# A fourth buffer for the weights' halves of a two-layer decoder trunk, with room from the descriptors' area and an ordering line for the casts

## The chip, the cores and the metric

The kernel runs on one core of a Trainium2 chip. The metric is the device time of one execution in microseconds. A core has five engines that work side by side, each through its own queue in order: PE (matrix multiplication), ACT (activations, copies, casts), DVE (elementwise work), POOL (elementwise work and the transfers that it issues) and SP (which here only issues transfers). An instruction that must wait for another engine waits for a semaphore, and holds what is queued behind it.

## The reference

Two identical layers over 512 tokens of width 1024. Each layer mixes tokens in four ways and adds the gated sum to x, then adds a SwiGLU block:

```python
def reference(x, positions, ln1, ln2, w_in, ...):
    cos, sin = rotary_tables(positions)
    for l in range(DEPTH):
        h = rms_norm(x, ln1[l])
        x = x + mixer_block(h, cos, sin, w_in[l], ...)
        h = rms_norm(x, ln2[l])
        x = x + swiglu(h, w_ffn_in[l], w_ffn_out[l])
    return x
```

`mixer_block` projects h to the inputs of a forgetting attention (fox), a gated linear attention (gla), a retention (ret) and a state-space scan (ssd) and to four gates; each mixer's result goes through an up projection, is multiplied by the sigmoid of its gate, and the sum goes through `w_out`. `swiglu` has a hidden width of 2816. All of it is float32.

## The kernel before, in words

**Precision.** A float32 product is made of three matmuls in a faster 32-bit format (`mm3`, L202): each operand is split into a high part, its cast, and a low part, the remainder. `split` (L213) does it with a cast on ACT (L214) and a subtraction on DVE (L215). The result is high by high, high by low and low by high.

**The stream of weights.** The weights lie in memory in the order of their use, cut into slabs of eight 128x128 blocks (a slab is 128x1024). `load` (L247) has SP transfer a slab into a tile `wr` (two buffers). `convert` (L259) splits it into `wh` and `wl`, tiles of the pool `wp` that `piece` (L158) makes: three buffers each. `ahead` and `block` (L270, L275) keep the conversion two slabs ahead of use: when PE's program reaches the first block of slab m, slab m+1 is converted, and slab m-1 is given up. The cast into `wh` of a slab has to wait for PE's last matmul on the slab three before, whose buffer it takes. A slab of full-width products is 24 matmuls of 512 columns.

**The stages of a layer.** A group of projections and the state-space, gla, ret and fox mixers come first. The mixers are generators (`ssd`, `gla`, `ret`, `fox`); between their steps `drain` inserts projections, gates and up projections from the list `fill`, so that PE has other work while ACT and DVE do a mixer's elementwise steps. `headnorm` ends gla and ret: squares, split, two matmuls with a constant matrix (tiles `mx` from `cr`), then Ln and Exp on ACT. In fox, `value` transposes the probabilities (L1082), splits them and multiplies them by the values. `ups` (L1163) multiplies an up projection by its gate on DVE (L1171). The second half of a layer is a Strassen scheme for the SwiGLU's input projection (`strassen`): `prep` makes the halves of a product's left operand with tiles from the same `wh` and the pool `lp`, `early` (L1286) makes a low part by a negated copy on ACT (L1289) and an accumulating transfer that POOL issues (L1290), and `collect` copies results out of a bank on ACT (L1352). The plain output projection follows in the slabs' way.

**What sets the order.** The code is recorded once, and then a scheduler puts each engine's instructions into an order, by dependences and by a cost model of its own (`schedule_with_timeline_sim=True`). `order(a, b)` (L222) adds a dependence that only this scheduler sees: a is put behind b in its reckoning, with no semaphore between them. It is used so far for activations and the loads of their tables.

**Memory.** At address 0 of every partition lies an area for the descriptors of POOL's transfers, 16384 bytes by default. The pools follow, `cp` first, then a gap, `wp`, a gap, and the rest. `piece` shifts a tile within its buffer for some slabs.

Of the kernel before, what the change touches and what calls it, by code (L numbers as in the profile page):

```python
# [11 lines left out]
F32R = mybir.dt.float32r  # L12
# [6 lines left out]
P = 128  # L19
# [16 lines left out]
SLAB = 8  # L36
# [98 lines left out]
def trunk(ctx: ExitStack, tc: tile.TileContext, keys, qkeys, xin, pos, wst, wsq, par, ext, cst, out):  # L135
    nc = tc.nc
    V, A, G, T = nc.vector, nc.scalar, nc.gpsimd, nc.tensor
# [3 lines left out]
    wp = ctx.enter_context(tc.tile_pool(name="wp", bufs=3))  # L141
# [9 lines left out]
    def nm(s):  # L151
        uid[0] += 1
        return f"{s}{uid[0]}"
# [2 lines left out]
        pool.tile([P, n // 4], F32, tag=nm("pad"), name=nm("pad"))  # L156

    def piece(tag, shift=0):  # L158
        t = wp.tile([P, SLAB * P + 64], F32R, tag=tag, name=nm(tag))
        return t[:, shift:shift + SLAB * P]  # L160

    pools = {}
# [34 lines left out]
        return ap.rearrange("p (c t) -> p c t", c=n)  # L197

    def mm(o, l, r, start, stop):
        T.matmul(o, lhsT=l, rhs=r, start=start, stop=stop, skip_group_check=True)  # L200

    def mm3(o, l, r, start, stop):  # L202
        (lh, ll), (rh, rl) = l, r
        mm(o, lh, rh, start, False)
        mm(o, lh, rl, False, False)
        mm(o, ll, rh, False, stop)
# [4 lines left out]
            mm(o, a, b, start and i == 0, stop and i == 1)  # L211

    def split(src, hi, lo):  # L213
        A.copy(out=hi, in_=src)  # L214
        V.tensor_tensor(out=lo, in0=src, in1=hi.bitcast(F32), op=ALU.subtract)  # L215
        return hi, lo

    def split_tile(t):
        return split(t, TT(F32R), TT(F32R))

    def split_small(t, shape, tag):
        return split(t, sp.tile(shape, F32R, tag=tag + "h", name=nm(tag), bufs=1), sp.tile(shape, F32R, tag=tag + "l", name=nm(tag), bufs=1))  # L222

    seen = {"set": None, "last": None}

    def order(a, b):
        tc.add_manual_dep(a.ins, b.ins.name, mybir.DependencyInfo(mybir.DependencyClass.NoSync, mybir.DependencyReason.DATA), reason="table")
# [13 lines left out]
            seen["last"] = i  # L241
        return i

    raw, ready = [], []
    cap = [SLABS]

    def load():  # L247
# [7 lines left out]
    def halves(n):  # L255
        w = SLAB * P
        return [slice(0, w // 2), slice(w // 2, w)] if n < 2 else [slice(0, w)]

    def convert():  # L259
        n = len(ready)  # L260
        if n < SLABS:
            far = n % (BLOCKS // SLAB) in TOKEN
            hi, lo = (piece("wh", 16), piece("wl", 48)) if far else (piece("wh"), piece("wl"))
            for h in halves(n):
                split(raw[n][:, h], hi[:, h], lo[:, h])
            ready.append((hi, lo))
            raw[n] = None

    def ahead(n):
        while len(ready) < min(SLABS, cap[0], n):  # L270
            if len(raw) == len(ready):
                load()
            convert()

    def block(*key, width=1):  # L275
        n = len(keys)
        if n % SLAB == 0:
            ahead(n // SLAB + AHEAD)
            if n // SLAB:
                ready[n // SLAB - 1] = None  # L280
        for i in range(width):
            keys.append(key[:-1] + (key[-1] + i * P,))
        i = n % SLAB
        hi, lo = ready[n // SLAB]
        sl = slice(i * P, (i + width) * P)
        return hi[:, sl], lo[:, sl]
# [139 lines left out]
    def group(name, l, cols, src, nk, hook=None):  # L426
        ps = [MX() for _ in cols]
        for k in range(nk):
            if hook and k == 4:
                hook()  # L430
            for i, c in enumerate(cols):
                mm3(ps[i], block(name, l, k, c), src[k], k == 0, k == nk - 1)
        return ps

    def proj(name, l, c, src, nk):
        ps = MM()
        for k in range(nk):
            mm3(ps, block(name, l, k, c), src[k], k == 0, k == nk - 1)
        return ps

    def layer(l, n1, scope):
# [72 lines left out]
        def tokmajor(dst, c, stacked=False):  # L514
            st = {}

            def go(half):
                def f():
                    if half == 0:
                        if not stacked:  # L520
                            dst.append(vp.tile([P, NB, 256], F32, tag="v", name=nm("v")))
                        st["ps"] = [MM(), MM()]
                    for k in range(4 * half, 4 * half + 4):
                        w = block("w_in", l, k, c, width=2)
                        assert (len(keys) - 1) // SLAB % (BLOCKS // SLAB) in TOKEN
                        for tb in range(NB):
                            ts = slice(tb * P, (tb + 1) * P)
                            o = st["ps"][tb // 2][:, (tb % 2) * 256:(tb % 2) * 256 + 256]
                            mm3(o, (n1.hi[:, k, ts], n1.lo[:, k, ts]), w, k == 0 and tb % 2 == 0, k == KD - 1)
                    if half:  # L530
                        for tb in range(NB):
                            v, rt = st["ps"][tb // 2][:, (tb % 2) * 256:(tb % 2) * 256 + 256], n1.rt[:, tb:tb + 1]
                            if stacked:
                                t = TT(F32R).rearrange("p (h s d) -> p h s d", h=NH, s=2)
                                v = v.rearrange("p (h d) -> p h d", h=NH)
                                act(out=t[:, :, 0], in_=v, func=AF.Copy, scale=rt)
                                V.scalar_tensor_tensor(out=t[:, :, 1], in0=v, scalar=rt, in1=t[:, :, 0].bitcast(F32), op0=ALU.mult, op1=ALU.subtract)
                                dst.append(t)
                            else:
                                act(out=dst[0][:, tb], in_=v, func=AF.Copy, scale=rt)  # L540
                return f
            return [(4.1, go(0)), (4.1, go(1))]
# [713 lines left out]
        def strassen(units):  # L1256
# [29 lines left out]
            def early(u, p):  # L1286
                t, j = st[u][OF[p]]
                lo = piece("wl", 32)
                A.activation(out=lo, in_=t, func=AF.Copy, scale=-1.0)  # L1289
                G.dma_start(out=lo, in_=wsq[j], accum_op=ALU.add)  # L1290
                st[u]["lo", p] = lo

            def prep(u, p):
                s = st[u]
                hi = piece("wh")
                if p in LATE:
                    A.copy(out=hi, in_=s[OF[p]][0])
                    s[p] = hi, s.pop(("lo", p))
                    return
                a11, a12, a21, a22 = (s[q][0] for q in ("11", "12", "21", "22"))  # L1300
                if p == 6:
                    s1 = wp.tile([P, SLAB * P], F32, tag="wr", name=nm("wr"), bufs=2)
                    s["s1"] = sub(s1, a21, a22, ALU.add)
                    sub(a21, a11, a21)
                    sub(a11, s1, a11)
                    s[p] = split(a11, hi, LT())
                    if u + 1 < len(units):
                        load(u + 1)
                    return
                if p == 3:  # L1310
                    sub(a12, a12, a11)
                t = {5: s["s1"], 7: a21, 3: a12}[p]
                s[p] = split(t, hi, LT())
# [139 lines left out]
    o, w = PAR_OFF["ln1"]  # L1453
# [78 lines left out]
```

## Time and profile before

| | |
|---|---|
| median of the runs shown (3) | 1709.49 us (1709.37 to 1709.84) |
| profiled execution | 1709.5 us |
| its span in the profile | 1707.8 us |
| granted TensorE clock, mean | 1.0 |
| busy: PE, DVE, ACT, POOL | 99%, 71%, 51%, 13% |

Durations are those of one profiled execution. A view of waits names the engine and line that waited, then what it waited for, the total, the count and the longest. A view of groups names line, engine, operation and tiles (out<-in, buffer numbers left out), then count, busy time, mean of one in ns, and the idle time before it. Matmuls overlap in the profile: the end of each is modelled, so idle time of PE is counted only from that end on. Lines are those of the kernel before; in the changed kernel they are up to three higher.

### The profile page before, as it was taken

The numbers are of one execution on the slowest core, as the hardware profiler recorded it, in microseconds if no ns is written. First come the engines' busy times: TensorE is split into PE (matmuls) and PEld (weight loads), VectorE is DVE, ScalarE is ACT, GpSimd is POOL, SyncE is SP. The second block draws the span as 40 slices with busy tenths as digits, with TensorE's granted clock in tenths as the row PEclk, the third lists the DMA queues.
The fourth block names the chain that finished last, engine by engine and source line by source line (L and its number), as shares of the span: only waits on it lengthen the run. The fifth ranks groups of instructions, "written<-read, shape, count | busy, mean of one in ns | idle before, by whom it ended". The sixth has DMA issues, their size and how long they took to land.

```text
span 1707.8 us, 25188 instructions
## 1 busy us (share of the span) xinstructions
PE 1695.8 (99%) x10164; PEld 1475.3 (86%) x10164; DVE 1215.3 (71%) x1691; ACT 863.5 (51%) x1190; POOL 216.8 (13%) x221
## 2 busy tenths in 40 slices
PE   8999999999999999999999999999999999999998
PEld 7878888888888999998988788888888889999997
DVE  6867676768677677676777666767776677767666
ACT  5435543546347646464544354435554474655643
POOL 3021220022101010101020212201221010101010
PEclk9999999999999999999999999999999999999999
DMA  5322222222235657575333222222222365665753
GB/s 206 100 74 75 75 87 75 87 87 74 88 110 141 193 133 188 136 184 120 92 100 111 73 75 75 90 81 89 76 85 87 99 177 160 152 176 139 186 105 105
DMA packets 54693, 195.00 MB, mean 114 GB/s; under 512 B 6064, under 2 KB 6448, under 8 KB 54576
## 3 DMA queue, kind: packets, MB, share of 16 engines
q1 hardware_dynamic: 45072, 160.45, 29.9%
q0 software_dynamic: 8640, 31.46, 10.4%
q8 instruction: 79, 1.29, 0.3%
q10 hardware_dynamic: 864, 1.48, 0.2%
q14 instruction: 38, 0.31, 0.1%
HBM read 191.28 MB, written 2.10 MB: 113 GB/s over the span
## 4 chain that ended last, share of the span: by engine, by line
PE 96%; DVE 1%; ACT 1%; DMA 1%; issue 0%; ACTq 0%; DVEq 0%
PE mm L200 65%; PE mx L200 31%; PE mx L1082 1%; DMA x<-in_x_dram 0%; DMA t<-in_ext_dram 0%; ACT wh L214 0%; DVE wl L215 0%; PE mx L692 0%; DVE t L372 0%; ACT L233 0%; DVE t L836 0%; ACT g L238 0%; DVE t L1171 0%; PE mx L954 0%; PE mx L871 0%
## 5 line engine op out<-in xcount | busy, mean ns | idle before, releaser
L214 ACT CAST wh<-wr 128x1024 fp32r<-128x1024 f32 (+1 forms) x240 | 250.1, 1043 | 359.8 <-PE mm L200 207.5
L200 PE MATMUL mm<-xh,wh 128*128 128x512 f32 (+1 forms) x1184 | 428.4, 362 | 1.4 <-DVE t L1171 0.9
L200 PE MATMUL mm<-xh,wl 128*128 128x512 f32 (+1 forms) x1184 | 427.5, 361 | 0.0
L200 PE MATMUL mm<-xl,wh 128*128 128x512 f32 (+1 forms) x1184 | 427.5, 361 | 0.0
L215 DVE TENSOR_TENSOR wl<-wr,wh 128x1024 fp32r<-128x1024 f32 (+1 forms) x220 | 285.6, 1300 | 110.3 <-ACT wh L214 108.0
L200 PEld LDWEIGHTS mm<-xh,wh 128*128 128x128 f32 x1184 | 222.4, 188 | 36.3 <-DVE t L1171 1.8
L200 PEld LDWEIGHTS mm<-xl,wh 128*128 128x128 f32 x1184 | 222.4, 188 | 34.4 <-issue 1.5
L200 PEld LDWEIGHTS mm<-xh,wl 128*128 128x128 f32 x1184 | 222.5, 188 | 33.8 <-issue 0.6
L200 PE MATMUL mm<-t,wh 128*128 128x512 f32 x448 | 140.3, 392 | 0.0
L200 PE MATMUL mx<-xh,wh 128*128 128x256 f32 (+1 forms) x448 | 136.1, 311 | 3.1 <-ACT wh L214 3.1
L200 PE MATMUL mx<-xl,wh 128*128 128x256 f32 (+1 forms) x448 | 138.3, 309 | 0.0
L1290 POOL DMA_DIRECT2D wl<-in_wsq_dram x60 | 52.0, 867 | 517.4 <-ACT wl L1289 416.4
L200 PE MATMUL mx<-f,wh 128*128 128x512 f32 x352 | 108.2, 390 | 0.0
L200 PE MATMUL mm<-f,wh 128*128 128x512 f32 x352 | 105.9, 389 | 0.0
L200 PEld LDWEIGHTS mm<-t,wh 128*128 128x128 f32 x448 | 83.2, 188 | 17.3
L215 DVE TENSOR_TENSOR l<-rq,wh 128x1024 fp32r<-128x1024 f32 x60 | 73.2, 1220 | 33.0 <-ACT wh L214 18.6
L200 PEld LDWEIGHTS mx<-xh,wh 128*128 128x128 f32 x448 | 84.0, 188 | 9.3 <-ACT wh L214 4.2
L200 PE MATMUL mx<-xh,wl 128*128 128x256 f32 (+1 forms) x288 | 91.0, 327 | 0.0
L200 PEld LDWEIGHTS mx<-xl,wh 128*128 128x128 f32 x448 | 84.1, 188 | 5.1
L200 PE MATMUL mm<-t,wl 128*128 128x512 f32 x224 | 87.4, 390 | 0.0
L214 ACT CAST wh<-rq 128x1024 fp32r<-128x1024 f32 x60 | 63.0, 1049 | 43.8 <-PE mm L200 21.5
L200 PEld LDWEIGHTS mm<-f,wh 128*128 128x128 f32 x352 | 66.1, 188 | 13.5
(275 smaller groups left out, 3428.6 us busy)
## 6 DMA issues: line engine op xcount, KB each, us to landing
wr<-in_wst_dram SPq DMA_DIRECT2D x216, 512.0 KB, 3.5
rq<-in_wsq_dram SPq DMA_DIRECT2D x60, 512.0 KB, 5.6
wl<-in_wsq_dram POOLq DMA_DIRECT2D x60, 512.0 KB, 6.8
wr<-in_wsq_dram SPq DMA_DIRECT2D x20, 512.0 KB, 6.8
out_dram<-x SPq DMA_DIRECT2D x8, 256.0 KB, 2.0
x<-in_x_dram SPq DMA_DIRECT2D x3, 512.0 KB, 6.7
wr<-in_wst_dram SPq DMA_DIRECT2D x4, 256.0 KB, 5.6
x<-in_x_dram SPq DMA_DIRECT2D x2, 256.0 KB, 4.5
```

Source lines behind the costliest of these rows:

```text
L200: T.matmul(o, lhsT=l, rhs=r, start=start, stop=stop, skip_group_check=True)
L214: A.copy(out=hi, in_=src)
L215: V.tensor_tensor(out=lo, in0=src, in1=hi.bitcast(F32), op=ALU.subtract)
L1082: T.transpose(ps[:, W:W + P], zs[qb][:, kb * P:(kb + 1) * P], ident)
L1290: G.dma_start(out=lo, in_=wsq[j], accum_op=ALU.add)
```

## The change

`wh` and `wl` get four buffers, which takes 2 x 4352 = 8704 bytes more of each partition; the descriptors' area falls from 16384 to 8192 bytes. A slab's cast now takes the buffer of the slab four before, so its semaphore wait is for that slab. In place of the shorter distance, `convert` adds a dependence of the cast on the last matmul recorded before slab n-2 was begun (kept in `spent`) by `order`, which the scheduler alone sees.

```diff
     def piece(tag, shift=0):
-        t = wp.tile([P, SLAB * P + 64], F32R, tag=tag, name=nm(tag))
+        t = wp.tile([P, SLAB * P + 64], F32R, tag=tag, name=nm(tag), bufs=4)
...
     def mm(o, l, r, start, stop):
-        T.matmul(o, lhsT=l, rhs=r, start=start, stop=stop, skip_group_check=True)
+        seen["mm"] = T.matmul(o, lhsT=l, rhs=r, start=start, stop=stop, skip_group_check=True)
...
-        A.copy(out=hi, in_=src)
+        seen["copy"] = A.copy(out=hi, in_=src)
...
-    raw, ready = [], []
+    raw, ready, spent = [], [], {}
...
             for h in halves(n):
                 split(raw[n][:, h], hi[:, h], lo[:, h])
+                if n - 3 in spent:
+                    order(seen["copy"], spent[n - 3])
...
             if n // SLAB:
                 ready[n // SLAB - 1] = None
+                spent[n // SLAB - 1] = seen["mm"]
...
-    nc = _bacc.Bacc("TRN2", target_bir_lowering=False, num_devices=1)
+    nc = _bacc.Bacc("TRN2", target_bir_lowering=False, num_devices=1, dynamic_dma_scratch_size=8192)
```

The scheduler gives every engine but POOL and SP a largely different order. Three places follow.

ACT at the end of retention in layer 0. Before (wh_2883 is the cast of a slab's high part, t_2736 to t_2744 are the squares of a head norm of the retention and their high parts):

```order
L238 ACTIVATE t_2730<-t_2288 128x512
L214 CAST wh_2883<-wr_2881 128x1024
L214 CAST t_2732<-t_2730 128x512
L238 ACTIVATE t_2736<-t_2335 128x512
L214 CAST wh_2921<-wr_2919 128x1024
L214 CAST t_2738<-t_2736 128x512
```

And now:

```order
L238 ACTIVATE t_2742<-t_2382 128x512
L214 CAST t_2744<-t_2742 128x512
L238 ACTIVATE t_2748<-t_2438 128x512
L214 CAST t_2750<-t_2748 128x512
L238 ACTIVATE t_2815<-mx_2803,cs 128x512
L238 ACTIVATE t_2817<-mx_2806,cs 128x512
L214 CAST wh_2883<-wr_2881 128x1024
L238 ACTIVATE t_2815<-t_2815 128x512
L214 CAST wh_2921<-wr_2919 128x1024
```

The cast of wh_2883 moved from ahead of the second square's high part to behind the activations that read the sums mx_2803 and mx_2806.

PE at the same place, now (mm_2918 is the projection that begins with that slab, mx_2806 to mx_2812 are the head norm's sums):

```order
L200 MATMUL mm_2902<-t_1489,wl_2851 128x512
L200 MATMUL mx_2806<-t_2739,cr 128x512
L200 MATMUL mx_2809<-t_2744,cr 128x512
L200 MATMUL mx_2809<-t_2745,cr 128x512
L200 MATMUL mx_2812<-t_2750,cr 128x512
L200 MATMUL mx_2812<-t_2751,cr 128x512
L200 MATMUL mm_2918<-xh_135,wh_2883 128x512
L200 MATMUL mm_2918<-xl_136,wh_2883 128x512
L200 MATMUL mm_2918<-xh_135,wl_2884 128x512
```

Before, the four matmuls on mx_2809 and mx_2812 stood among those of mm_2918; now they come ahead of all of these.

ACT at the entry of the Strassen scheme in layer 0. Before (e_4909 and e_4911 are copies of a product's two banks, mm_4883 and mm_4884; n_4839 is the second norm's factor):

```order
L233 ACT_TABLE_LOAD
L1352 COPY e_4909<-mm_4883 128x256
L214 CAST wh_4864<-rq_4764 128x1024
L1289 ACTIVATE wl_4880<-rq_4872 128x1024
L1409 COPY f_4848<-mx_4669 128x512
L1409 COPY f_4848<-mx_4671 128x512
L214 CAST wh_4913<-wr_4865 128x1024
L1352 COPY e_4911<-mm_4884 128x256
```

And now:

```order
L214 CAST wh_4913<-wr_4865 128x1024
L1292 ACTIVATE wl_4951<-wr_4770 128x1024
L238 ACTIVATE n_4839<-mm_4832,cs 128x512
L1355 COPY e_4909<-mm_4883 128x256
L238 ACTIVATE n_4839<-n_4839 128x512
L233 ACT_TABLE_LOAD
L214 CAST wh_4947<-rq_4768 128x1024
L1355 COPY e_4911<-mm_4884 128x256
```

The cast of wh_4913 moved ahead of the norm's factor, and another cast came in between the load of the table and the copy of the second bank, which PE overwrites with the next product; on PE, this next product (mm_4884 from t2h_4664) now follows directly on that of mm_4883, where four other matmuls and more stood between before.

PE in a head of fox, in layer 0, now (mx_3787 and mx_3847 are transposed probabilities, mm_3878 is a gate's projection, mx_3691 takes the product with the values, t_3792 and t_3793 are the high and the low part of mx_3787):

```order
L1085 MATMUL mx_3787<-cs,t_3751 128x128
L1085 MATMUL mx_3787<-cs,t_3680 128x128
L1085 MATMUL mx_3787<-cs,t_3751 128x128
L1085 MATMUL mx_3847<-cs,t_3751 128x128 x2
L200 MATMUL mm_3878<-xh_135,wl_3805 128x512
L200 MATMUL mx_3691<-t_3792,t_2590 128x256
L200 MATMUL mx_3691<-t_3793,t_2590 128x256
```

And before:

```order
L1082 MATMUL mx_3787<-cs,t_3751 128x128
L1082 MATMUL mx_3787<-cs,t_3680 128x128
L1082 MATMUL mx_3787<-cs,t_3751 128x128
L1082 MATMUL mx_3847<-cs,t_3751 128x128 x2
L200 MATMUL mm_3937<-t_2694,wh_3865 128x512
L200 MATMUL mm_3937<-t_2695,wh_3865 128x512
L200 MATMUL mm_3937<-t_2694,wl_3866 128x512
```

Between the transposes and the product with the values there is now one matmul, where a whole run of projections stood before.

## The prediction

> **What bounds the kernel now.** I read the page first, then the waits of PE and of ACT, then the timeline at the places that the new order touches. The page (busy us, share, instructions; then the chain that ended last) says that PE is the path from end to end:
>
> ```profile
> span 1707.8 us, 25188 instructions
> PE 1695.8 (99%) x10164; PEld 1475.3 (86%) x10164; DVE 1215.3 (71%) x1691; ACT 863.5 (51%) x1190; POOL 216.8 (13%) x221
> PE 96%; DVE 1%; ACT 1%; DMA 1%; issue 0%; ACTq 0%; DVEq 0%
> ```
>
> The waits of PE (engine, line, waited for: us in total, times, longest) are short, and two rows, POOL and most of the ACT one, belong to the first 20 us:
>
> ```profile
> PE mx L200 <- ACT wh L214: 3.1, 3, 1.7
> PE mm L200 <- POOL t L328: 1.4, 1, 1.4
> PE mx L200 <- DVE t L215: 1.2, 2, 0.7
> PE mm L200 <- DVE t L1171: 0.9, 2, 0.5
> PE mm L200 <- DVE t L489: 0.5, 1, 0.5
> ```
>
> ACT, half idle, waits much for PE in front of the weights' casts:
>
> ```profile
> ACT wh L214 <- PE mm L200: 229.0, 94, 7.5
> ACT wh L214 <- PE mx L200: 56.1, 38, 8.5
> ```
>
> So a change can win only what PE waits, and it can lose wherever PE arrives at a weight or a bank before ACT and DVE are done. To price that I need the spacing of work in the queues. From the timeline (start, us, engine, line, names):
>
> ```profile
> 316.68 0.62 ACT L214 CAST t<-t 128x512 fp32r<-128x512 f32 x1
> 317.06 0.62 PE L200 MATMUL mm<-t,wh 128*128 128x512 f32 x2
> 317.20 0.63 ACT L238 ACTIVATE t<-t 128x512 f32<-128x512 f32 x1
> 317.33 0.69 DVE L215 TENSOR_TENSOR t<-t,t 128x512 fp32r<-128x512 f32 x1 [0.74 <-ACT t L214]
> ...
> 427.85 0.71 PE L1082 MATMUL mx<-cs,t 128*128 128x128 f32 x5
> ...
> 428.32 0.71 PE L200 MATMUL mm<-t,wh 128*128 128x512 f32 x2
> 428.38 0.59 ACT L214 CAST t<-mx 128x512 fp32r<-128x512 f32 x1 [1.55 <-PE mx L1082]
> ...
> 548.14 0.28 PE L200 MATMUL mm<-xh,wl 128*128 128x256 f32 x1
> ...
> 548.37 0.28 PE L200 MATMUL mm<-xl,wh 128*128 128x256 f32 x1
> ```
>
> Two matmuls of 512 columns take 0.62 us, of which the last takes 0.39 by the model (row below): one starts 0.23 after the other, and its end lies 0.16 after the next could start. For 256 columns it is 0.115 (two spacings in 0.23). Five transposes start within 0.47: 0.09 each. The pair behind the transposes took 0.71 instead of 0.62: changing between the two kinds costs 0.09. ACT starts its next instruction 0.52 after one of 0.62: 0.10 overlap. DVE starts 0.03 after the cast that it needs ends. For the first instruction behind a PE end I take 0.04, for PE behind ACT or DVE 0.05; these two are estimates near that 0.03.
>
> **The change part by part.** Durations (xcount, busy us, mean ns, idle before):
>
> ```profile
> L200 PE MATMUL mm<-xh,wh 128*128 128x512 f32 x864 | 339.9, 393 | 1.4 <-DVE t L1171 0.9 <-DVE t L489 0.5
> L200 PE MATMUL mm<-t,wh 128*128 128x512 f32 x448 | 140.3, 392 | 0.0
> L1082 PE MATMUL mx<-cs,t 128*128 128x128 f32 x80 | 15.0, 274 | 0.0
> L200 PE MATMUL mx<-t,t 128*128 128x384 f32 x24 | 7.4, 350 | 0.0
> L214 ACT CAST wh<-wr 128x1024 fp32r<-128x1024 f32 x236 | 247.8, 1051 | 359.8 <-PE mm L200 207.5 <-DMA wr<-in_wst_dram 71.7 <-PE mx L200 39.8
> L214 ACT CAST wh<-rq 128x1024 fp32r<-128x1024 f32 x60 | 63.0, 1049 | 43.8 <-PE mm L200 21.5 <-PE mx L200 16.2 <-DVE rq L1280 5.5
> L233 ACT ACT_TABLE_LOAD x40 | 51.3, 1283 | 0.7
> L238 ACT ACTIVATE t<-mx,cs 128x512 f32<-128x512 f32 x16 | 10.5, 683 | 7.5 <-PE mx L200 7.5
> L238 ACT ACTIVATE t<-mx 128x384 f32<-128x384 f32 x8 | 3.7, 491 | 9.5 <-PE mx L200 9.5
> L214 ACT CAST t<-mx 128x512 fp32r<-128x512 f32 x8 | 4.7, 587 | 20.3 <-PE mx L1082 20.3
> L1352 ACT COPY e<-mm 128x256 f32<-128x256 f32 x120 | 42.6, 369 | 30.0 <-PE mm L200 29.9
> L1289 ACT ACTIVATE wl<-wr 128x1024 fp32r<-128x1024 f32 x20 | 21.4, 1070 | 0.0
> L238 ACT ACTIVATE n<-mm,cs 128x512 f32<-128x512 f32 x4 | 2.7, 686 | 3.3 <-PE mm L200 3.3
> L238 ACT ACTIVATE n<-n 128x512 f32<-128x512 f32 x8 | 5.1, 633 | 0.3
> L215 DVE TENSOR_TENSOR wl<-wr,wh 128x1024 fp32r<-128x1024 f32 x216 | 282.0, 1306 | 110.2 <-ACT wh L214 108.0 <-PE mx L200 1.5
> L215 DVE TENSOR_TENSOR t<-mx,t 128x512 fp32r<-128x512 f32 x8 | 5.5, 692 | 14.4 <-ACT t L214 14.4
> L1171 DVE TENSOR_TENSOR t<-mm,g 128x512 f32<-128x512 f32 x64 | 43.5, 682 | 24.6 <-PE mm L200 21.6 <-PE mx L1082 2.9
> ```
>
> *The fourth buffer* removes the semaphore wait of a cast on PE (the 229.0 + 56.1 us). By itself that is worth nothing to PE, since ACT's idle time hides it. *The ordering line* holds no engine at run time, but it tells the scheduler that a cast belongs behind a matmul, and so casts move back in ACT's queue, behind activations. What then stands ahead of a cast waits itself for PE's most recent work. In five kinds of place I compare the chain with what PE still has to issue.
>
> 1. End of retention, both layers. ACT: the activation on mx_2806, then wh_2883. From the start of the last mx_2806 matmul: 0.39 + 0.04 + (0.68 - 0.10) + 1.05 + 0.05 = 2.11 us until PE may use wh_2883. PE has 5 matmuls, 5 x 0.23 = 1.15: it waits 0.96. Two matmuls later it needs the low part: 0.04 + 1.31 + 0.05 = 1.40 behind the cast, of which 0.05 + 0.46 are gone: 0.89 more. 1.85 twice: +3.7.
> 2. Values of fox, once per layer. PE now uses the split of mx_3787 one matmul after the transposes. Chain from the third transpose: 0.27 + 0.04 + 0.59 + 0.03 + 0.69 + 0.05 = 1.67 to the low half. PE: three transposes 0.27, a main matmul 0.23, one of 256 columns on the high half 0.115: 0.62. +1.05 twice: +2.1.
> 3. Same stage, a merge product (L1171 of before, t_3103) now stands on DVE behind transposes, and the next projection needs its bank: 0.27 + 0.04 + 0.68 + 0.05 = 1.04 against 3 x 0.09. +0.77 twice: +1.5.
> 4. Entry of the Strassen stage. From the matmul that frees the slot of wh_4913, ACT does cast, negated copy, Ln, bank copy, Exp, table load, cast, bank copy: 1.05 + 1.07 + 0.69 + 0.37 + 0.63 + 1.28 + 1.05 + 0.37 = 6.51, less five overlaps of 0.10, and 0.39 + 0.04 + 0.05 around it: 6.49. PE issues 4 matmuls of 512 and 36 of 256 columns: 0.92 + 4.14 = 5.06, and then overwrites that bank. +1.43 twice: +2.9.
> 5. State-space stage of layer 0: wh_1093 stands behind three activations on scores. 0.35 + 0.04 + 3 x (0.49 - 0.10) + 1.05 + 0.05 = 2.66 against four matmuls of 384 columns (0.17 by their length) and four of 512: 1.60. +1.06: +1.1.
>
> PE's own order changes kind 193 times where it did 181 times: 12 x 0.09 = +1.1. What goes: in the same stretches the wait on L1171 (0.9 idle and twice 0.16) and the one on L489 (0.5 + 0.16), since PE is held elsewhere first: -1.9. The waits on L215 stay. Sum: 3.7 + 2.1 + 1.5 + 2.9 + 1.1 + 1.1 - 1.9 = +10.5 us.
>
> Two things have no row. Low parts that queue on DVE behind a maximum that waits for POOL (wl_3866) cost between 0 and 0.9 per layer: I take 0 and leave 1.9 for the upper end. The memory move: what lies ahead of the weights shifts by 8192 bytes, what lies behind by 512. The two rows of 512 columns differ by 1 ns with their operands (393 and 392); 1 ns on half of PE's 10164 matmuls would be 5.1 us either way. I take 0, since both shifts are multiples of 512.
>
> **The rivals.** (a) *The buffers were the limit.* ACT no longer stands in front of casts, activations come earlier, and all PE waits behind the start vanish: 1.2 + 0.9 + 0.5 idle and five times 0.16, -3.4 us: 1706.1. For it: the 285 us of ACT. Against it: PE shows 2.6 us of such idle time in all. The Trainium skill ("Perfetto Trace Analysis", Identifying Performance Opportunities) says that gaps which keep repeating on the engine that should be saturated can mean too little SBUF for the next tile. By that rule the time would be this rival's; but the repeating gaps stand on ACT at 51%, not on PE at 99%, so the trace does not bear it out. Chance 0.04.
> (b) *Casts are late only in the order.* Released from PE, ACT runs ahead, weights are ready, and the switches and lost waits are all: +1.1 - 1.9, 1708.7. It decides wherever what stands ahead of a cast needs nothing recent of PE. Against it: in places 1, 4 and 5 the cast's predecessor does. Chance 0.08.
> (c) *Worse*: DVE falls behind as well, or the addresses cost: 10.5 + 1.9 + 5.1 gives 1727.0. Chance 0.07.
> (d) *The halved descriptor area holds POOL up.* POOL's transfers and their queue:
>
> ```profile
> q0 software_dynamic: 8640, 31.46, 10.4%
> L1290 POOL DMA_DIRECT2D wl<-in_wsq_dram x60 | 52.0, 867 | 517.4 <-ACT wl L1289 416.4
> ```
>
> The 60 transfers are 8640 packets, 144 each. With half the room for descriptors, one of them might wait for an earlier one; were each held by a quarter of a microsecond on the path, +15 with nothing else, 1724.5. Against it: POOL stands idle for 416.4 us in front of them, waiting for ACT, so it could take up a hold of this size. Chance 0.03.
>
> **How the numbers follow.** The profiled execution took 1709.5 us (span 1707.8), the median of the runs is 1709.49, so the sum applies to either: 1709.5 + 10.5 = 1720.0. Chance of the forecast, slower by 4 to 15: 0.78. A measurement can tell 0.2%, 3.4 us. Slower: 0.78 + 0.07 + 0.03 = 0.88; same (b): 0.08; faster (a): 0.04. The range: below, the added waits reduced by half (12.4 / 2 = 6.2, since an estimate of 0.04 here and a matmul there is worth much in such differences) gives +4.3, 1713.8; I go to 1713.5. Above, 1.9 for DVE and 3.1 of the 5.1: 1725.0.
>
> **What would show it.** PE's waits for ACT wh L214 and DVE wl L215 appear behind the start, some 4 us and more together, near 320 and 1170 us, and for the copy e of L1352 (three lines later now) near 550 and 1400; ACT's waits of wh on PE fall from 285 us to below 100; busy time of PE stays near 1696. Wrong would be: PE waits for weights only in the first 20 us, or an unchanged order of waits with longer matmuls, which would be the addresses.

## The result and the profile after

| | before | after |
|---|---|---|
| median of 4 runs | 1709.66 us | 1727.55 us (1727.46 to 1728.33) |
| ratio | | 1.0106, 95% interval 1.0093 to 1.0119 |
| profiled span | 1707.8 us | 1725.9 us |

The kernel became 17.9 us slower. Slower was forecast, with 1720.0 us and a range up to 1725.0; the loss is larger than that. The head of the page after, as that of before was shown (busy us, share, instructions):

```profile
span 1725.9 us, 25117 instructions
PE 1709.9 (99%) x10164; PEld 1481.5 (86%) x10164; DVE 1208.1 (70%) x1691; ACT 860.6 (50%) x1190; POOL 215.4 (12%) x221
```

The same 10164 matmuls are busy for 14.1 us more (1695.8 before). That is the first thing to see: PE's added idle time is only some 4 us, and most of the loss is hidden in "busy". PE's waits after:

```profile
PE mm L200 <- ACT e L1355: 2.6, 2, 1.3
PE mm L200 <- ACT wh L214: 2.0, 3, 0.8
...
PE mx L200 <- DVE t L215: 1.2, 4, 0.3
PE mm L200 <- DVE t L1174: 1.1, 2, 0.6
PE mm L200 <- DVE wl L215: 1.1, 2, 0.5
PE mx L200 <- ACT t L214: 0.5, 2, 0.2
```

Before, no row named a cast or a low part of a weight behind the start, and none a bank copy `e`. Now rows name all three, and the wait on L489 is gone. ACT in return waits less for PE in front of the casts, 160.0 us instead of 285.1:

```profile
ACT wh L214 <- PE mm L200: 122.0, 64, 4.7
ACT wh L214 <- PE mx L200: 38.0, 27, 7.9
```

The end of retention in layer 0 in the timeline (start, us, engine, line, names; in brackets the idle time and its releaser):

```profile
320.92 1.33 PE L200 MATMUL mx<-t,cr 128*128 128x512 f32 x5
...
321.36 0.69 ACT L238 ACTIVATE t<-mx,cs 128x512 f32<-128x512 f32 x1 [0.20 <-PE mx L200]
321.95 1.03 ACT L214 CAST wh<-wr 128x1024 fp32r<-128x1024 f32 x1
...
323.02 1.23 DVE L215 TENSOR_TENSOR wl<-wr,wh 128x1024 fp32r<-128x1024 f32 x1 [1.11 <-ACT wh L214]
...
323.04 0.50 PE L200 MATMUL mm<-xh,wh 128*128 128x512 f32 x1 [0.78 <-ACT wh L214]
...
324.30 0.50 PE L200 MATMUL mm<-xh,wl 128*128 128x512 f32 x1 [0.53 <-DVE wl L215]
```

The cast stands behind the activation on a sum that PE has just finished, PE has five matmuls in that time, and then it stands idle twice. With 0.16 for the modelled end of the matmul before, these are 0.95 and 0.70 us; 0.96 and 0.89 were forecast. The entry of the Strassen stage:

```profile
552.89 0.69 ACT L238 ACTIVATE n<-mm,cs 128x512 f32<-128x512 f32 x1
553.47 0.37 ACT L1355 COPY e<-mm 128x256 f32<-128x256 f32 x1
553.73 0.64 ACT L238 ACTIVATE n<-n 128x512 f32<-128x512 f32 x1
554.39 1.28 ACT L233 ACT_TABLE_LOAD   x1
555.68 1.04 ACT L214 CAST wh<-rq 128x1024 fp32r<-128x1024 f32 x1
556.63 0.37 ACT L1355 COPY e<-mm 128x256 f32<-128x256 f32 x1
...
557.05 0.39 PE L200 MATMUL mm<-t2h,wh 128*128 128x256 f32 x1 [1.30 <-ACT e L1355]
```

ACT works through its queue without a pause, and PE waits for the last copy, 1.30 + 0.16; 1.43 was forecast. So the waits came where they were forecast and at their size, yet 1727.5 isn't 1720.0. What the sum lacked shows in the starts of single matmuls. These are the 256-column matmuls of the first Strassen group, PE alone:

```profile
573.44 0.28 PE L200 MATMUL mx<-xh,wh 128*128 128x256 f32 x1
...
574.39 0.28 PE L200 MATMUL mx<-xh,l 128*128 128x256 f32 x1
574.51 0.28 PE L200 MATMUL mm<-xh,wl 128*128 128x256 f32 x1
...
575.19 0.28 PE L200 MATMUL mm<-xh,wl 128*128 128x256 f32 x1
```

Eight steps lie between 573.44 and 574.39, 0.119 us each; six between 574.51 and 575.19, 0.113 each. Nothing waits here. PE has two cadences (times from one start to the next) for the same kind of product, and it changes from one to the other in the middle of the stage. After, the first 12 us of each of the later groups and some 21 us of the first group of a layer run in the slow one; before, about one us and some 5. Two windows of 8 us in the second group of layer 0, after (window, length, PE busy and matmuls, granted clock, DMA share, GB/s):

```profile
626.00:634.00 8.00, 8.00 (x70) 1.00 0.90 181
640.00:648.00 8.00, 8.00 (x73) 1.00 0.81 157
```

Both are 100% busy at the full clock (1.00), with 70 matmuls in one and 73 in the other; in the kernel before, both have 73. Over all 256-column matmuls of the weight products, the time between two starts adds up to 4.6 us more than before.

Both cadences stood in the trace before already. In the mixers, the products of 256 columns with a weight as the left operand came every 0.118 us throughout (94 in a row from 163.24 to 174.31), and their rows had a longer mean (one of them is shown) than those of the Strassen products, 276 to 278 ns:

```profile
L200 PE MATMUL mm<-wh,xl 128*128 128x256 f32 x128 | 36.3, 283 | 0.0
```

The other new place is PE's state steps of the gated linear attention, 64-column matmuls with the state `sbd`. After:

```profile
210.59 1.70 PE L200 MATMUL mx<-t,sbd 64*64 64x64 f32 x26
...
212.88 0.32 PE L200 MATMUL mx<-t,sbd 64*64 64x64 f32 x2
213.14 0.50 PE L200 MATMUL mm<-t,wl 128*128 128x512 f32 x1
213.47 0.63 PE L200 MATMUL mm<-t,wh 128*128 128x512 f32 x2
214.03 0.33 PE L200 MATMUL mx<-t,sbd 64*64 64x64 f32 x2
```

From then on they come in pairs between projections. Each pair holds PE for 0.26 us (212.88 to 213.14), and the projection behind it takes 0.33 (213.14 to 213.47) instead of 0.23. The projection ahead of a pair takes 0.10 longer too: the two from 213.47 to 214.03 take 0.56 instead of 0.46. Over both layers the steps stand in 13 runs, where they stood in 2. The unbroken run is shown with e6 below. The parts of the sum, measured from the starts of the matmuls, in us over both layers:

| term | forecast | measured |
|---|---|---|
| 1 end of retention | 3.7 | 3.3 |
| 2 values of fox | 2.1 | 2.2 |
| 3 merge product | 1.5 | 1.5 |
| 4 Strassen entry | 2.9 | 2.9 |
| 5 state-space stage | 1.1 | 0.9 |
| waits that went | -1.9 | -3.2 |
| changes of kind, small steps | 1.1 | about 5 |
| slow cadence | not seen | 4.6 |

The waits that went are the two on L1171 and the one on L489 (1.9), and also the two on L215 in fox, from 0.70 and 0.82 to 0.40 each, and two of 0.3 near 193 and 1039 us. Of the 18.1 us by which the span grew, 5.9 are left when the other rows are taken off; e6 measures 4.8 for the small steps by themselves, and some 1 stays unassigned.

### The profile page after: what moved, and what is told of

It reads as the page before. It is cut to its first block, busy times and chain, and to the rows that moved or that the text cites. A ratio compares the mean times of both kernels' runs of the same rounds, so it can differ in the third digit from the quotient of the medians.

```text
span 1725.9 us, 25117 instructions
## 1 busy us (share of the span) xinstructions
PE 1709.9 (99%) x10164; PEld 1481.5 (86%) x10164; DVE 1208.1 (70%) x1691; ACT 860.6 (50%) x1190; POOL 215.4 (12%) x221
## 3 DMA queue, kind: packets, MB, share of 16 engines
q10 hardware_dynamic: 864, 1.48, 0.2%
## 4 chain that ended last, share of the span: by engine, by line
PE 96%; ACT 2%; DVE 1%; issue 0%; DMA 0%; ACTq 0%; DVEq 0%
PE mm L200 65%; PE mx L200 30%; DVE sbd L898 0%; PE mx L1085 0%; ACT wh L214 0%; DVE wl L215 0%; ACT n L238 0%; ACT L233 0%; PE mx L695 0%; DMA x<-in_x_dram 0%; ACT t L238 0%; DVE t L215 0%; ACT xh L238 0%; ACT wl L1292 0%; PE mx L957 0%
## 5 line engine op out<-in xcount | busy, mean ns | idle before, releaser
L214 ACT CAST wh<-wr 128x1024 fp32r<-128x1024 f32 (+1 forms) x240 | 247.9, 1042 | 285.6 <-DMA wr<-in_wst_dram 162.3
L215 DVE TENSOR_TENSOR wl<-wr,wh 128x1024 fp32r<-128x1024 f32 (+1 forms) x220 | 276.1, 1261 | 104.8 <-ACT wh L214 71.1
L215 DVE TENSOR_TENSOR l<-rq,wh 128x1024 fp32r<-128x1024 f32 x60 | 73.3, 1222 | 50.3 <-PE mm L200 16.0
L1359 DVE TENSOR_TENSOR f<-mx,e 128x256 f32<-128x256 f32 x120 | 48.9, 420 | 54.9 <-PE mx L200 42.9
L214 ACT CAST wh<-rq 128x1024 fp32r<-128x1024 f32 x60 | 62.9, 1049 | 45.9 <-PE mm L200 33.9
```

The source lines that it names most:

```text
L214: seen["copy"] = A.copy(out=hi, in_=src)
L1359: V.tensor_tensor(out=s["t"][g][:, i, cols], in0=s[bank][g][:, :H], in1=s.pop((n, g)), op=ALU.add)
```

## The experiments

The theory after the result: (A) the ordering line makes the waits in the mixers and breaks up the small steps, because it moves casts behind other work in ACT's queue; (B) the fourth buffer by itself makes the wait at the Strassen entry and the slow cadence, because PE then gets the first Strassen product as one whole run instead of a part early; (C) addresses and descriptors cost nothing. The rivals are the addresses for the 4.6 us, and one of line and buffer alone for everything. Each kernel ran 4 to 11 times:

| run | median us | lowest to highest | ratio to before, 95% interval |
|---|---|---|---|
| e1 addresses only | 1709.48 | 1709.22 to 1710.04 | 1.0000 (0.9991 to 1.0009) |
| e2 buffer alone | 1719.08 | 1718.18 to 1720.76 | 1.0054 (1.0041 to 1.0067) |
| e3 line alone | 1722.77 | 1722.01 to 1723.05 | 1.0074 (1.0062 to 1.0087) |
| e4 after, first product apart | 1723.48 | 1722.88 to 1724.26 | 1.0081 (1.0067 to 1.0095) |
| e5 buffer, line at retention | 1722.57 | 1720.72 to 1724.57 | 1.0078 (1.0064 to 1.0092) |
| e6 buffer, line in gla | 1722.97 | 1722.09 to 1728.40 | 1.0083 (1.0071 to 1.0096) |
| e7 buffer, line in fox | 1722.05 | 1721.09 to 1722.23 | 1.0071 (1.0058 to 1.0083) |
| e8 buffer, mended | 1729.34 | 1728.44 to 1731.52 | 1.0117 (1.0103 to 1.0130) |
| e9 buffer, first product apart | 1716.18 | 1714.88 to 1719.59 | 1.0043 (1.0029 to 1.0056) |
| e10 before, first product apart | 1709.80 | 1709.42 to 1711.08 | 1.0002 (0.9993 to 1.0010) |
| e11 line with another anchor | 1719.96 | 1719.72 to 1720.01 | 1.0061 (1.0047 to 1.0074) |

The kernel before took 1709.51 to 1709.57 beside them (medians). Single runs of some kernels with four buffers differ by 2.6 to 6.3 us, so a difference of 3 us between two of these medians is read together with the waits and the starts in the traces.

**e1, the addresses.**

```diff
+            pad(wp, 8704)
             for g, n in zip(gap, (32, 256)):
...
-    nc = _bacc.Bacc("TRN2", target_bir_lowering=False, num_devices=1)
+    nc = _bacc.Bacc("TRN2", target_bir_lowering=False, num_devices=1, dynamic_dma_scratch_size=8192)
```

> The kernel before in its own order, three buffers, but with the descriptors' area of 8192 bytes and 8704 bytes of padding ahead of the weights' pool, so that everything outside that pool lies where it lies in the changed kernel. Theory 'cadence from the order': the addresses cost nothing, 1709.5 us within 0.5, and the 256-column products of the Strassen stage keep 113 ns. Rival 'addresses': the 4.6 us that these products lost came from the memory move, 1714 us, with the products at 119 ns for the first 12 us of a group. A third, the halved descriptor area alone: over 1711 us with POOL's transfers landing later.

Measured: 1709.48. The same window as above, in e1:

```profile
626.00:634.00 8.00, 8.00 (x73) 1.00 1.04 269
```

73 matmuls. So neither the memory move nor the halved area costs anything, and the prediction's 0 for the addresses and its rival (d) are settled by one experiment: that rival wanted +15 from the area alone.

**e2 and e3, buffer alone and line alone.** e2 is the changed kernel without the line:

```diff
-                if n - 3 in spent:
-                    order(seen["copy"], spent[n - 3])
```

e3 is the kernel before with the line, `bufs=4` and the smaller area taken back.

> The changed kernel without the ordering line: four buffers and the smaller descriptor area, nothing else. Theory 'two causes': the waits at the end of retention (1.65 us a layer) and in the values of fox go with the line, the wait for the bank copy at the Strassen entry (1.46 us a layer) and the slow cadence of the 256-column products (4.6 us) belong to the buffer and stay: 1709.5 + 2.9 + 4.6, less 0.7 for the removed wait near 110 us, 1716 us within 1.5. Rival 'the line does it all': no new wait and 1709.5 us or less. Rival 'the buffer does it all': 1727 us.

> The kernel before with the ordering line alone: three buffers, the larger descriptor area. Theory 'two causes': the waits at the end of retention (1.65 us a layer), in the values of fox (1.1) and in the state-space stage (0.9 once) appear with three buffers too, the Strassen entry has no new wait, and the 256-column products stay at 113 ns because the first of a group is still started apart from the rest: 1709.5 + 2 x 1.65 + 2 x 1.1 + 0.9 and some 3 for more changes of the matmuls' kind and waits of small matmuls, 1719 us within 2. Rival 'the line only repeats the buffer's own wait': the casts may not run ahead of the buffer anyway, so nothing changes, 1709.5 us.

Measured: 1719.08 and 1722.77. PE's waits in e2 (lines one or two lower there):

```profile
PE mm L200 <- ACT e L1353: 2.9, 3, 1.3
...
PE mx L200 <- DVE xl L399: 0.9, 1, 0.9
PE mm L200 <- DVE t L1172: 0.9, 2, 0.5
PE mm L200 <- DVE t L490: 0.5, 1, 0.5
```

The copy `e` stands first, and the old waits on L1171 and L489 stand as before: up to the Strassen entry, e2 keeps within 0.2 us of the kernel before. The buffer does nothing at all for the mixers. In the Strassen stage it has the same slow stretches as the changed kernel, 4.7 us in all. It is 3 us above the forecast; 1.5 of these are two waits that the changed kernel doesn't have, near 811 us for a copy and near 875 us for the low part of a normalised x (the row on L399), and 0.7 is the wait on L489, which was expected to go and stayed. PE's waits in e3:

```profile
PE mx L200 <- DVE t L933: 2.3, 2, 1.3
PE mm L200 <- ACT wh L214: 2.0, 3, 0.8
...
PE mm L200 <- DVE wl L215: 1.1, 2, 0.5
PE mx L200 <- ACT t L214: 0.4, 2, 0.2
```

Casts and low parts again, and no copy `e`. The rows of `mm` on wh L214 and wl L215 are those of the changed kernel to the digit. The line thus makes the mixers' waits with three buffers too. A wait of e3's own comes in, for a step of a rotation (L933), 2.7 by the starts; without it e3 would lie within the 2 us of its forecast of 1719, and with it it lies 3.8 above. The buffer by itself loses 9.5 and the line by itself 13.2, but both in one kernel lose 17.9: each has waits of its own (1.5 and 2.7 by the starts) that the changed kernel doesn't have.

**e4, the slow cadence.** In the changed kernel the first Strassen product of each group is begun in another sequence. Everything on ACT, DVE, POOL and SP stays in its order.

```diff
+                lone = (u, p) == (0, 1)
+                if lone:
+                    for g in range(2):
+                        sl = slice(HK * g * P, (HK * g + 1) * P)
+                        mm(bank[g][:, :H], hi[:, sl], rh[:, 0], True, False)
+                        mm(bank[g][:, :H], hi[:, sl], rl[:, 0], False, False)
                 for g in range(2):
                     for k in range(HK):
                         sl = slice((HK * g + k) * P, (HK * g + k + 1) * P)
+                        if lone and k == 0:
+                            mm(bank[g][:, :H], lo[:, sl], rh[:, 0], False, False)
+                            continue
```

> The changed kernel, with the first Strassen product of each group begun in another sequence: its first two steps on each of its two banks come first, then the rest; the same matmuls, and the other four engines as they were. Theory 'cadence from the order': a break in the three-step sequence takes PE out of the slow cadence, so the 256-column products run at 113 instead of 119 ns from the first product on: 1727.5 - 4 us, 1723.5 us within 1. Rival 'addresses' or 'a wait that the profile does not show': 1727.5 us within 0.5, products at 119 ns as before.

Measured: 1723.48, 4.1 below the changed kernel, as expected. The windows in e4:

```profile
626.00:634.00 8.00, 8.00 (x73) 1.00 0.89 190
640.00:648.00 8.00, 8.00 (x73) 1.00 0.90 163
```

Both are now fast; the slow stretches of all eight groups are gone but for a few matmuls. The traces of the two kernels have the same instructions in the same order on all four other engines. The same matmuls on the same data lose 4 us by nothing but the sequence in which a stage is entered.

**e5, e6, e7, the line in one stage at a time**, each against e2:

```diff
-                if n - 3 in spent:
+                if n - 3 in spent and (n % (BLOCKS // SLAB) in (49, 50)):
```

and `30 <= n % (BLOCKS // SLAB) <= 42` in e6, `52 <= ... <= 75` in e7.

> Four buffers with the ordering line at two casts a layer only, wh_2883 and wh_2921 of layer 0 and their like of layer 1, against e2 (four buffers, no line, 1719.1 us). Theory 'a late cast is a wait on PE': the waits at the end of retention come back at their full size (0.95 + 0.70 a layer) and with them the merge product's (0.73 a layer), the wait on L1171's product there (0.62 a layer) goes: +3.5 us, 1722.6 within 0.8. Rival 'only the sum of all moved casts slows PE, by contention': two casts of 240 change nothing, 1719.1 us.

> Four buffers with the ordering line only at the casts of the slabs 30 to 42 of a layer (the gated linear attention), against e2 (1719.1 us). No activation stands newly ahead of a cast with PE waiting for it there, but PE's state steps of 64 columns now alternate with projections, with 18 more changes of kind. Theory 'a broken chain of small steps costs twice': changes at 0.09 to 0.11 each (1.9 us) and steps that wait for the state on DVE (in the changed kernel the 64-column steps took 8.1 instead of 3.8 us) together 4 us, 1723 within 1. Rival 'changes of kind alone': +1.9, 1721. Rival 'no weight is late, so nothing': 1719.1.

> Four buffers with the ordering line only at the casts of the slabs 52 to 75 of a layer (the fox stage), against e2 (1719.1 us). Theory 'a late cast is a wait on PE': the waits in the values of fox (1.09 a layer) and on the merge product (0.73 a layer) come back, the wait on L215 falls by 0.3 a layer, small ones add 0.3 a layer: +3.6, 1722.7 us within 1. Rival: these waits in the changed kernel followed from what retention did before them and not from the line here: 1719.1.

Measured: 1722.57 (+3.5), 1722.97 (+3.9), 1722.05 (+3.0); by the spans of the profiled executions +3.2, +5.3 and +3.7. PE's waits in e5:

```profile
PE mm L200 <- DVE t L1174: 1.1, 2, 0.6
PE mm L200 <- ACT wh L214: 1.1, 2, 0.5
PE mm L200 <- DVE wl L215: 1.1, 2, 0.5
```

Two casts a layer, put behind a matmul in the scheduler's reckoning, bring back the waits for wh, for wl and for the merge product (L1174 is L1171 of before); that for wh is 0.71 a layer by the starts, not the 0.95 expected. In e7 the split of the values and the merge product wait again:

```profile
PE mm L200 <- DVE t L1174: 2.0, 4, 0.6
...
PE mx L200 <- ACT t L214: 0.5, 2, 0.2
```

e6 has no new wait worth a row in the mixers. The state steps of layer 0 in e2, and then in e6:

```profile
210.94 1.92 PE L200 MATMUL mx<-t,sbd 64*64 64x64 f32 x56
```

```profile
211.29 0.92 PE L200 MATMUL mx<-t,sbd 64*64 64x64 f32 x13
...
213.04 0.32 PE L200 MATMUL mx<-t,sbd 64*64 64x64 f32 x2
213.30 0.50 PE L200 MATMUL mm<-t,wh 128*128 128x512 f32 x1
```

In one run, 56 steps take 1.92 us, 0.034 each, a pair 0.07. Apart, a pair takes 0.26 (213.04 to 213.30), and the matmul ahead of it and the one behind it 0.10 more each. PE does other work between the pairs, and the figures are nearly the same at each pair, which speaks against waits for DVE, which makes the state. Followed matmul by matmul to the end of the mixers, e6 falls 2.0 us behind e2 in layer 0 and 2.8 in layer 1. That is most of the "about 5" of the table, and 18 changes of kind at 0.1 each would be 1.8 of it. Behind the mixers the first Strassen group of layer 0 is without its slow stretch in e6, 0.8 less, and a copy is waited for near 1668 us, 1.1 more.

The three runs together lose 10.4 us to the line, where it costs 8.5 in the changed kernel (1727.55 - 1719.08); the merge product's wait, 1.5, is in both e5 and e7.

**e8 and e9, can the buffer be had without its costs?** e8 is e2 with e4's edit, and with the casts of Strassen's halves ordered behind the bank copies; e9 is e2 with e4's edit alone.

```diff
-                        A.copy(out=s[n, g], in_=s["a"][g][:, :H])
+                        seen["e"] = A.copy(out=s[n, g], in_=s["a"][g][:, :H])
...
+                    if seen.get("e"):
+                        order(seen["copy"], seen["e"])
```

> Four buffers, no line, with the first Strassen product of each group begun apart as in e4, and the casts of Strassen's halves ordered behind the last bank copies recorded, against e2 (1719.1 us). Theory 'two costs of the buffer': the slow cadence goes (-4.1) and the wait at the Strassen entry becomes shorter, since one cast of 1.05 stands less ahead of the copy while Exp and the table load still do (1.49 to some 0.9, -1.1): 1714 us within 1; the two single waits of e2 near 811 and 875 us (1.5 together) may go too, 1712.4. Rival 'the buffer gains something once its costs are gone': under 1709 us.

> Four buffers, no line, with the first Strassen product of each group begun apart as in e4 and nothing else: it parts e8's two edits. Theory 'the slow cadence is worth 4 us wherever it stands, and e8's own ordering lost the rest': 1719.1 - 4.1 = 1715.0 us within 1, with the wait for the bank copy at the Strassen entry as in e2 (1.5 a layer). Rival 'the break itself costs e8 its waits': 1725 us or more.

Measured: 1729.34 and 1716.18. e9 gains 2.9 of the 4.1 (3.4 by the spans of the profiled executions) and comes out just above its range, 1715.0 within 1; the first group of each layer, which has the wait for the copy in it, stays slow for 17 us behind that wait. e8 came out 15 us above its forecast, and its waits say how:

```profile
PE mx L200 <- DVE f L1372: 7.1, 6, 1.6
PE mm L200 <- ACT e L1368: 2.0, 2, 1.0
```

The new ordering of the casts moved the products about, and PE now waits for the additions that empty the other banks (L1372). The wait that it was to shorten by 1.1 fell from 1.48 and 1.51 to 1.18 in each layer by the starts, 0.6 together. It is the same error as that of the change, made once more: a dependence that only the scheduler sees was meant for one place and rearranged a stage.

**e10, the kernel before with e4's edit.**

> The kernel before with the first Strassen product of each group begun apart, nothing else. Before, a group is slow for 8 products' matmuls only, and the first group of a layer for some 40: 0.5 us in all is to be had. Theory 'cadence': 1709.1 us within 0.5, not to be told from before. Rival 'the slow cadence belongs to a stage': no change at all, or slower where the break makes the entry slow again.

Measured: 1709.80, no difference that the runs could show (0.9993 to 1.0010). Before, there is next to nothing slow in the Strassen stage to remove, some 0.8 us by the starts.

**e11, another anchor.** The line puts a cast behind the last matmul that reads the slab three before, not behind the last matmul of any kind:

```diff
-                if n - 3 in spent:
-                    order(seen["copy"], spent[n - 3])
+                for x in spent.get(n - 3, ()):
+                    if x in used:
+                        order(seen["copy"], used[x])
```

(`used` holds the last matmul that read a tile, `spent` the slab's two tiles.)

> The changed kernel with another anchor for the line: a cast is put behind the last matmul that reads the parts of the slab three before, no longer behind the last matmul of any kind recorded before the next slab began. Theory 'any line reshuffles the casts': the waits at the end of retention go, but a head of fox waits for its values' split in another place (0.7 + 0.6 a layer by the order), and PE changes kind 18 times more than with four buffers alone: 1719.1 + 2.6 + 1.9, 1723.6 us within 1.5. Rival 'the anchor was too late': with the right anchor the line repeats what three buffers enforced, the mixers run as before, and only the buffer's own costs stay: 1719.1 us within 1.

Measured: 1719.96, within the rival's figure. Its mechanism isn't what happened, though. The mixers don't run as before; PE's waits are

```profile
PE mm L202 <- ACT e L1361: 2.6, 2, 1.3
...
PE mx L202 <- ACT t L219: 0.9, 2, 0.5
```

with the split of a head's values (L219 is L214 of before) in another place, 0.5 and 0.6 a layer by the starts, as the theory had it. The small steps of the gated linear attention are broken up here as well, into 10 runs: from each of their starts to the next matmul's they take 6.0 us in all, and 3.6 in e2. Against these stand waits that are shorter than in e2: the two of 811 and 875 us are gone, that on L1171 fell from 0.62 to 0.40 a layer. And the first Strassen group of each layer is fast behind its wait here, which saves some 1.5 us. So the rival's figure was met by costs and gains that happen to cancel. The anchor matters, 7.6 us between two choices of it, but no choice tried gives the order of before back.

The best version with four buffers, e9, is 6.6 us slower than the kernel before.

## Why the prediction was right and wrong

**Right: the bound and the mechanism.** PE was the path, ACT's 285 us of waiting in front of the casts were worth nothing (they fell to 160 while the kernel got slower), and rival (a) with its 1706.1 has nothing left. Two signs had the right direction and the wrong size: these 285 us were to fall below 100, and PE's waits for wh and wl behind the start add up to 3.1 us, not some 4 and more. Casts moved back in ACT's queue, and PE waited for them, which rules out rival (b), 1708.7.

**Right: the five places and their prices.** 11.3 us were summed from single rows, 10.8 were measured, each place within 0.4 us. e5 and e7 bring back places 1, 2 and 3, the merge product (3) in both of them; place 4 stands in e2, and place 5 in e3, by the starts near 113 us.

**Half right: which edit makes which wait.** The prediction put all five to the ordering line. e2 and e3 show that the Strassen entry belongs to the buffer and the rest to the line.

**Right: the zeros.** Memory move 0 (e1), late low parts in fox 0 (no such wait after).

**Wrong: "PE's own order changes kind 193 times where it did 181 times: 12 x 0.09 = +1.1".** The failure lies in the price: it was that of one change, from short matmuls to long ones, behind a run. In the gated linear attention the changes cut a run of small steps into pairs, and there an interruption costs 0.39 us: a pair at 0.26 instead of 0.07, and 0.10 each on the matmul ahead of it and the one behind it. Eleven more of them are 4.3 us (an estimate from these steps); e6 measures 4.8 for the stage in both layers. The trace before has the run of 56 steps in 1.92 us; set beside the new order, it tells where a cost of this kind must come, though not its size.

**Wrong: that the duration of a matmul is a constant of its row.** "Busy time of PE stays near 1696" failed by 14.1 us. The sum took the spacing of 256-column matmuls at 0.115 everywhere, though the trace before has both 0.113 and 0.118, and the range had no case in which it changes but the addresses of rival (c). The 4.6 us came from the order in which a stage is entered, as e4 shows by giving 4.1 of them back. Rival (c) came to 1727.0 and so close to the result, but by luck: 5.1 of it were the addresses, which cost nothing in e1, and 1.9 the late low parts in fox, which don't wait.

**The waits that went** were 3.2 and not 1.9, since waits on L215 became shorter too, which were to stay, and two small ones went. Without this third error the miss would have been larger.

What stays open is why PE has the two cadences and what switches them. In the traces a whole run of products, with the three steps always in the same sequence, kept the slow one for 100 matmuls and more; a product begun in two pieces ended it. A wait sometimes brought it back (e9) and sometimes didn't (e4, e11), and in e6 it did in one layer and not in the other. That is a description and no cause. Why a pair of small steps costs the matmuls beside it 0.10 each is open as well.

## What to carry to other kernels

A dependence that only a scheduler sees isn't a small edit: it reorders whole engines, and each place where the new order brings a producer next to its consumer is a wait that no edit in the diff shows. So the order is to be read place by place, on PE too, and runs of small matmuls are to be looked for there first. When busy time of a saturated engine grows with the same instructions, compare the starts of equal instructions in a stage before looking for waits.

## What the runs showed of the hardware

- The same 256-column matmuls came every 0.113 us or every 0.119 us, for stretches of 12 us and more, at the same granted clock of 1.00; which one depended on the sequence in which the stage was entered (e4). The Trainium skill ("TensorE: Matmul & The Clock Gate", Back-to-back issue gap) gives N / 2.4 + 2.5 ns at the full clock for an isolated one, which makes 109.2 ns for 256 columns (an estimate by that formula), and says that in a stream of loads and matmuls both set the spacing. The traces have two spacings, and neither is that value; the measurement decides.
- Small matmuls of 64 columns follow each other every 0.034 us in a run of 56. A pair between projections of 512 columns held PE for 0.26 us, and the projections ahead of it and behind it took 0.33 instead of 0.23.
- Halving the area for POOL's descriptors and moving nearly all of memory changed the time by less than 0.1% (0.9991 to 1.0009).
